# First products of an encoder layer taken from the unnormalised input, with the norm's scale put on their results

## The chip, the cores and the metric

The kernel runs on one core of a Trainium2 chip. The metric is the time on the device in microseconds (us) of one execution. The core has a tensor engine (PE, with its weight loads as PEld), a vector engine (DVE), a scalar engine (ACT), GpSimd (POOL), a sync engine (SP) that here only issues transfers, and DMA queues: those that SP issues on, and those that ACT issues on.

## The reference

Two layers of an encoder over 272 tokens (16 meta tokens and 256 of the input) of width 1024. What matters here is the head of a layer:

```python
def rms_norm(x, gain):
    y = x * lax.rsqrt(jnp.mean(x * x, axis=-1, keepdims=True) + EPS)
    return y * gain

for layer in range(DEPTH):
    hn = rms_norm(h, norm_mix[layer])
    proj = hn @ w_in[layer]        # queries, keys, values, SSM input, pooling input, gates
    ...                            # attention, SSM and pooling, merged: h = h + merged @ w_out
    hn = rms_norm(h, norm_mlp[layer])
    h = h + jnp.square(jax.nn.relu(hn @ w_up[layer])) @ w_down[layer]
return rms_norm(h, norm_final)[:, N_META:]
```

The factor rsqrt(...) is one number for each token, so it can be put on `x * gain` or on the product of `x * gain` with a weight matrix.

## The kernel before

Activations lie transposed: `h` is [128, 8, 272], eight blocks of 128 features by 272 tokens. Every product is made at float32's precision out of three matmuls in a rounded format (fp32r): an operand is split into a rounded part and the rest (`xh` and `xl` for activations, `hi` and `lo` for weights), and `product()` issues hi by xh, hi by xl, lo by xh for each of eight 128x128 blocks, 24 matmuls for a 128x1024 chunk of weights.

`need(i)` serves the weights. It asks for chunks up to three ahead on SP's queue (`raw`, three buffers), and splits up to two ahead: `hi` is an ACT copy (L169), `lo` a DVE subtraction (L170). `proj()` multiplies one chunk of `w_in`: first four SSM input products (results `pju`), then the keys (`pjk`), the values (`pjv`), four query products (`pjq`), pooling inputs, gates. Keys and queries go through a rotation (`rope`, with a small matmul `swk` or `swq`).

The norm at the start (before the loop over layers): five warm-up products (`warm`), the squares of the eight blocks of `h` as they arrive (`sqs`, seven on ACT in L898, one on DVE in L896), and `stats("m0")`: eight products with a matrix of ones add them up over the features (`ss_m`), ACT makes a first 1/sqrt (L294), and three short steps on ACT and DVE refine it (`nx_m`, `nt_m`, L301 `rstd_m`). Then for each block k DVE makes `xn` = h * rstd (L907), ACT `xh` (L908) and DVE `xl` (L912), both with the gain from `vecs`. These stand in program order on DVE by a `pin`, two blocks and then one weight split at a time.

Beside this main stream run generators ("side work") that `pump()` steps through: the SSM's parameters of the first layer are some hundred small DVE operations on 128x32 tiles (`scratch`), followed by wider ones (`gt`, `dd`, `b`); later the SSM scans, attention, pooling. The order of instructions on each engine is fixed when the program is built, by a scheduler that takes priorities and estimates of time; `issue_after` holds side work back until a given instruction. At run time an engine goes through its list in order, and an instruction that waits holds all behind it.

The four results `pju` are copied out of PSUM by ACT (`scaled`, L936, into `ue`) and sent to DRAM (`ud`), from where the scans load them. In the second layer the kernel already takes the first two SSM products before their scale is known: it keeps them (`uk`) and multiplies with rstd on DVE (L940).

Of the kernel before, what the change touches and what calls it, by code (L numbers as in the profile page):

```python
# [20 lines left out]
KT = 8  # L21
# [11 lines left out]
# how the side work is woven into the main stream of products: its rate per slot,  # L33
# by generator and layer, and the slots between a step and the product that uses it
# [23 lines left out]
AHEAD = 3  # chunks of weights loaded ahead of their use  # L58
SPLIT = 2  # and split
WARM = 5  # products that warm the tensor engine up  # L60
# [4 lines left out]
# polynomials, highest power first: e^r on +-ln(2)/2, sine and cosine on +-pi/4  # L65
# [5 lines left out]
# columns of the constant table  # L71
# [3 lines left out]
# columns of the SSM operands of eight groups  # L75
# [9 lines left out]
def encoder(ctx: ExitStack, tc: tile.TileContext, a: dict, out: bass.AP):  # L85
# [5 lines left out]
    class TE:  # L91
        """The tensor engine; side work does not overtake what is written before it."""
# [64 lines left out]
    WHOLE = {(0, 0), (0, 2)}  # (layer, branch) multiplied in float32 without a split  # L157
    raws = []

    def need(i, pinned=False):  # L160
        for j in range(len(raws), min(i + AHEAD + 1, len(chunks))):
            raws.append(wp.tile([P, 8, P], F32, tag="raw", name=f"raw{j}", bufs=3))
            SY.dma_start(raws[j][:, : chunks[j][0].shape[1], :], chunks[j][0])
        for j in range(len(made), min(i + SPLIT + 1, len(chunks))):
# [14 lines left out]
    def first_need(k):  # L179
        """The first chunks, split one by one."""  # L180
        need(k - SPLIT, pinned=True)

# [7 lines left out]
    ORDER = ((0, 1, 2, 3), (2, 3, 0, 1))  # SSM quarters; the last operands made are still on chip  # L190
# [28 lines left out]
    side = []  # L219

    class Side:
        """Steps of a generator, each yielding its cost and the slots it has to wait after it;
        a slot of the main stream allows it `rate`."""
# [24 lines left out]
    def pump(boost=0.0):  # L248
        """Side work for one slot of the main stream."""
        for e in list(side):  # L250
            e.run(boost or e.rate)
# [20 lines left out]
    def feed(n, k, t0):  # L272
        """Scaled, split copy of h's k-th block, and its squares; the last are returned apart."""
# [11 lines left out]
    def stats(name, t0, parts=None):  # L285
        """1/rms of every token, on all partitions; `parts`' squares are still to be summed."""
# [28 lines left out]
    def exp_acc(x):  # L315
        """e^x for x clamped to [-170, 100], to float32's accuracy."""
# [19 lines left out]
    def twice(c, s, co, so, w):  # L336
        """Cosine and sine of twice the angle."""
# [16 lines left out]
    def ssm_params(l):  # L354
# [4 lines left out]
        m5 = st(5)  # mag^4, mag^3, mag^2, mag, 1  # L359
# [49 lines left out]
        ct, sn = st(4), st(4)  # cosines and sines of 1..4 times the angle  # L409
# [12 lines left out]
        # f = (abar - 1) / lambda  # L422
# [13 lines left out]
        # the factors by half quarter and part: f's real part, and its imaginary part signed  # L436
# [3 lines left out]
        # input side: mag^(3-j) e^(-i (j+1) theta) f, rows in the order  # L440
        # (step, quarter, parity, pair), the steps from the last to the first
# [30 lines left out]
        # powers of abar on the output side  # L472
# [15 lines left out]
    def prepare(l, q, bun):  # L488
        """The SSM operands of the groups 8q..8q+7 of layer l."""
# [16 lines left out]
        # rotations by j times the chunk's angle, and the decay of a chunk  # L506
# [15 lines left out]
        # output matrices: [part, group, power, channel]; power 0 is C itself  # L522
# [17 lines left out]
        # input matrices, rows (parity, channel, step), columns (direction, state),  # L540
        # and between them the response within a chunk
# [69 lines left out]
    def prep(l):  # L611
        """Parameters and operands of layer l's SSM, ahead of the layer that uses them."""
# [16 lines left out]
    def scan_quarter(l, q):  # L629
# [22 lines left out]
        # four runs of chunks: real part's halves, imaginary part's halves in reverse  # L652
# [8 lines left out]
        for hb in range(2):  # L661
            # no group crosses the border of a bank
# [18 lines left out]
        # states before each chunk; the chunks run backward on the last 64 partitions  # L681
# [32 lines left out]
        # rotated back, [part, group, chunk], and all chunks put in order  # L714
# [16 lines left out]
        # outputs, rows (parity, step, channel)  # L731
# [23 lines left out]
    cold = []  # quarters whose results are long out  # L755
# [9 lines left out]
    def attention(l, kr, qr, vt, waits):  # L765
# [7 lines left out]
        for gi, (q0, w, mk) in enumerate(groups):  # L773
            yps = pm.tile([P, 512], F32, tag="yps", name=f"yps{l}{gi}", bufs=1)
            n = 4 if w == P else 1
            hw = 2 * w  # columns of two heads
# [103 lines left out]
    with tc.high_priority():  # L880
        params_load(0, S)
        for k in range(4):
            SY.dma_start(h[:, 2 * k : 2 * k + 2, :], a["h0"][:, 2 * k : 2 * k + 2, :])
        S.dma_start(consts[:, C_ONE : C_ONE + P], a["consts"][:, C_ONE : C_ONE + P])
        S.dma_start(vecs, a["vecs"])
        # the tensor engine reaches its full clock while h arrives
# [5 lines left out]
        parts = []  # L892
        sqs = slots(4, "sqs")
        for k in range(KT):
            if k == 1:
                V.tensor_tensor(sqs[:, k], h[:, k], h[:, k], ALU.mult)  # L896
            else:
                S.activation(sqs[:, k], h[:, k], AF.Square)  # L898
            parts.append(sqs[:, k])
        rstd, ia, iv = stats("m0", 0, parts)  # L900
# [416 lines left out]
```

## Time and profile before

| | us |
|---|---|
| median of three runs | 893.82 (893.33 to 897.0) |
| span of the profiled execution | 892.9 |
| PE busy | 870.0 (97%) |
| DVE busy | 675.3 (76%) |
| ACT busy | 541.0 (61%) |
| POOL busy | 4.1 (0%) |

The profiled execution's own time is not among the numbers at hand; its span lies 0.9 us below the median of the runs, which is what start and end take. The page's slices show PE at 9 tenths or more nearly everywhere, with the one low slice at the start; there also DVE and the granted clock are to be read, in microseconds rather than in slices.

### The profile page before, as it was taken

Reading aid. Unit: us, or ns where it says so; the run is one execution under the profiler, and the core shown is the slowest. Engines: PE = TensorE matmul, PEld = TensorE weight load, DVE = VectorE, ACT = ScalarE, POOL = GpSimd, SP = SyncE. Lnnn points to the kernel's source line nnn. Section 1 sums busy time; section 2 is a strip of 40 time slices with the busy share of each in tenths; the row PEclk is TensorE's granted clock in tenths of the full one; section 3 lists DMA queues with packets and bytes.
Section 4 is the critical chain, followed back from the end, with each engine's and each line's share of the span. In section 5 each row is a group of like instructions: output and inputs, shape, how many; then the busy total and the mean of one; then the engine's idle time right before and its main releaser. Section 6 shows DMA issues by size and latency. Waiting matters only on the chain.

```text
span 892.9 us, 18412 instructions
## 1 busy us (share of the span) xinstructions
PE 870.0 (97%) x7174; PEld 814.8 (91%) x7174; DVE 675.3 (76%) x1443; ACT 541.0 (61%) x1005; POOL 4.1 (0%) x32
## 2 busy tenths in 40 slices
PE   6999999999999999999999999999999999999995
PEld 4987777899899999999999988789999999999995
DVE  7987978899986557677896988677878755555564
ACT  5568597845567655477565467575565775357652
POOL 1000000000000000000000000000000000000000
PEclk7999999999999999999999999999999999999998
DMA  7644645454475556958766464625565565555551
GB/s 250 203 154 129 191 117 164 151 159 152 154 228 170 177 169 194 294 187 264 230 201 182 130 215 150 206 96 157 174 192 170 175 193 182 186 185 186 189 189 48
DMA packets 62520, 159.47 MB, mean 179 GB/s; under 512 B 20064, under 2 KB 25952, under 8 KB 62432
## 3 DMA queue, kind: packets, MB, share of 16 engines
q1 hardware_dynamic: 59696, 155.63, 55.8%
q10 hardware_dynamic: 2736, 2.65, 0.9%
q8 instruction: 56, 0.92, 0.4%
q14 instruction: 32, 0.26, 0.1%
HBM read 150.79 MB, written 7.47 MB: 177 GB/s over the span
## 4 chain that ended last, share of the span: by engine, by line
PE 79%; DVE 12%; ACT 4%; DMA 3%; issue 2%; DVEq 0%; ACTq 0%; SPq 0%
PE up L96 21%; PE dn L96 21%; PE pjg L96 10%; PE br L96 5%; PE wo L96 5%; DVE lo L170 3%; PE pju L96 3%; PE s L96 2%; PE pjp L96 2%; PE yps L96 1%; PE pt L101 1%; PE pjq L96 1%; PE l L96 1%; PE tp L96 1%; ACT hi L169 1%
## 5 line engine op out<-in xcount | busy, mean ns | idle before, releaser
L170 DVE TENSOR_TENSOR lo<-raw,hi 128x1024 fp32r<-128x1024 f32 x240 | 292.8, 1221 | 131.4 <-ACT hi L169 128.6
L169 ACT ACTIVATE hi<-raw 128x1024 fp32r<-128x1024 f32 x240 | 253.8, 1058 | 227.6 <-PE dn L96 75.2
L96 PE MATMUL dn<-hid,hi 128*128 128x272 f32 (+1 forms) x1024 | 188.0, 285 | 0.0
L96 PEld LDWEIGHTS dn<-hid,hi 128*128 128x128 f32 x1024 | 159.1, 188 | 0.1
L96 PE MATMUL up<-xh,hi 128*128 128x272 f32 (+1 forms) x512 | 146.2, 286 | 0.0
L96 PE MATMUL dn<-hid,lo 128*128 128x272 f32 (+1 forms) x512 | 146.1, 285 | 0.0
L96 PE MATMUL up<-xh,lo 128*128 128x272 f32 (+1 forms) x512 | 146.0, 285 | 0.0
L96 PE MATMUL up<-xl,hi 128*128 128x272 f32 (+1 forms) x512 | 145.9, 285 | 0.0
L96 PE MATMUL pjg<-xh,hi 128*128 128x272 f32 (+1 forms) x384 | 113.8, 296 | 0.0
L96 PE MATMUL pjg<-xh,lo 128*128 128x272 f32 (+1 forms) x384 | 111.2, 290 | 0.0
L96 PE MATMUL pjg<-xl,hi 128*128 128x272 f32 (+1 forms) x384 | 111.0, 289 | 0.0
L96 PEld LDWEIGHTS up<-xl,hi 128*128 128x128 f32 x512 | 96.3, 188 | 0.5 <-DVE xl L276 0.4
L96 PEld LDWEIGHTS up<-xh,hi 128*128 128x128 f32 x512 | 96.5, 189 | 0.3
L96 PEld LDWEIGHTS up<-xh,lo 128*128 128x128 f32 x512 | 96.6, 189 | 0.0
L96 PEld LDWEIGHTS dn<-hid,lo 128*128 128x128 f32 x512 | 96.5, 188 | 0.0
L96 PEld LDWEIGHTS pjg<-xh,hi 128*128 128x128 f32 x384 | 73.0, 190 | 4.9 <-issue 3.9
L96 PEld LDWEIGHTS pjg<-xh,lo 128*128 128x128 f32 x384 | 73.1, 190 | 2.1 <-issue 2.0
L96 PEld LDWEIGHTS pjg<-xl,hi 128*128 128x128 f32 x384 | 72.9, 190 | 1.8 <-issue 1.5
L96 PE MATMUL wo<-mgh,hi 128*128 128x272 f32 (+1 forms) x128 | 36.6, 287 | 0.6 <-ACT hi L169 0.6
L96 PE MATMUL wo<-mgh,lo 128*128 128x272 f32 (+1 forms) x128 | 36.2, 285 | 0.3 <-DVE lo L170 0.3
L96 PE MATMUL wo<-mgl,hi 128*128 128x272 f32 (+1 forms) x128 | 36.2, 285 | 0.1
L1167 ACT ACTIVATE rs<-re 128x272 f32<-128x272 f32 (+1 forms) x64 | 27.1, 424 | 1.8
(351 smaller groups left out, 1635.9 us busy)
## 6 DMA issues: line engine op xcount, KB each, us to landing
raw<-in_w_in_dram SPq DMA_DIRECT2D x76, 512.0 KB, 3.5
raw<-in_w_up_dram SPq DMA_DIRECT2D x64, 512.0 KB, 4.2
raw<-in_w_dn_dram SPq DMA_DIRECT2D x64, 512.0 KB, 4.0
raw<-in_w_br_dram SPq DMA_DIRECT2D x24, 512.0 KB, 4.0
raw<-in_w_out_dram SPq DMA_DIRECT2D x16, 512.0 KB, 3.7
b<-in_b_row_dram SPq DMA_DIRECT2D x16, 256.0 KB, 5.0
b<-ffd SPq DMA_DIRECT2D x16, 256.0 KB, 4.6
raw<-in_glu_w_dram SPq DMA_DIRECT2D x4, 512.0 KB, 4.3
```

Source lines behind the costliest of these rows:

```text
L96: i = nc.tensor.matmul(*args, **kw)
L101: i = nc.tensor.transpose(*args, **kw)
L169: S.activation(_r(hi), raws[j], AF.Copy)
L170: i_ = V.tensor_sub(_r(lo), raws[j], hi)
L1167: S.activation(sq, re, AF.Square)
```

## The change

Everything is at the start of the first layer.

- The first chunk of weights is requested first on SP's queue, ahead of the four pieces of `h`.
- `rawh` and `rawl` are made from `h` as it comes in: the rounded part of h * gain on ACT and the rest on DVE, the latter pinned. The first four products use them in place of `xh` and `xl`.
- The squares are summed over the eight blocks before the product with ones: ACT squares all eight, GpSimd adds seven times into `ssq`, and one product with ones remains.
- `u0` and `u1` are kept by ACT copies until rstd is there; all four results are multiplied with rstd on DVE (where ACT copied them before).
- `xn`, `xh`, `xl` are still made for all eight blocks, behind rstd, without a pin; keys, values and queries use them.
- `issue_after` and the extra steps of side work at the start (`first_pumps`) are gone.

```diff
-    def need(i, pinned=False):
+    def need(i, pinned=False, load=False):
         for j in range(len(raws), min(i + AHEAD + 1, len(chunks))):
             raws.append(wp.tile([P, 8, P], F32, tag="raw", name=f"raw{j}", bufs=3))
             SY.dma_start(raws[j][:, : chunks[j][0].shape[1], :], chunks[j][0])
+            if load:
+                return None
...
+    rawh, rawl = slots(0, "rawh"), slots(4, "rawl")
     with tc.high_priority():
         params_load(0, S)
+        need(0, load=True)
         for k in range(4):
             SY.dma_start(h[:, 2 * k : 2 * k + 2, :], a["h0"][:, 2 * k : 2 * k + 2, :])
...
-        parts = []
-        sqs = slots(4, "sqs")
+        first_need(0)
         for k in range(KT):
-            if k == 1:
-                V.tensor_tensor(sqs[:, k], h[:, k], h[:, k], ALU.mult)
-            else:
-                S.activation(sqs[:, k], h[:, k], AF.Square)
-            parts.append(sqs[:, k])
-        rstd, ia, iv = stats("m0", 0, parts)
+            S.activation(_r(rawh[:, k]), h[:, k], AF.Copy, scale=gain(0, k))
+            pin(V.scalar_tensor_tensor(
+                _r(rawl[:, k]), h[:, k], gain(0, k), rawh[:, k], ALU.mult, ALU.subtract
+            ))
...
-    ctx.enter_context(tc.issue_after(ia))
...
-    with tc.issue_after(iv):
-        for k in range(0, KT, 2):
-            xn = first(k), first(k + 1)
-            if k < 6:
-                first_need(k // 2)
-            second(k, xn[0])
-            second(k + 1, xn[1])
     Side(prep(0), PREP0)
     pump(BOOST)
-    first_pumps(iv)
+
+    def first_stats():
+        for k in range(KT):
+            if k == 0:
+                S.activation(ssq, h[:, k], AF.Square)
+            else:
+                sq = tmp(f"sq{k}")
+                S.activation(sq, h[:, k], AF.Square)
+                PO.tensor_tensor(ssq, ssq, sq, ALU.add)
+        return stats("m0", 0)[0]
+
+    def normed():
+        for k in range(KT):
+            xn = tmp(f"xn{k}")
+            V.tensor_tensor(xn, h[:, k], rstd, ALU.mult)
+            S.activation(_r(xh[:, k]), xn, AF.Copy, scale=gain(0, k))
+            V.scalar_tensor_tensor(
+                _r(xl[:, k]), xn, gain(0, k), xh[:, k], ALU.mult, ALU.subtract
+            )
...
-            ps = proj(plans[l, "in"][i], name=f"u{q}")
-            if l and i < 2:
+            ps = proj(plans[l, "in"][i], name=f"u{q}", given=xraw)
+            if i < 2:
                 if i == 0:
-                    rstd_l = stats(f"m{l}", 0, [ssq, sq7])[0]
+                    rstd_l = stats(f"m{l}", 0, [ssq, sq7])[0] if l else first_stats()
...
+                    if l == 0:
+                        normed()
```

The order on the engines moves with it. DVE before, at the end of the norm (names as above, `lo` with the number of its tile): the split of the activations starts here, two blocks and one weight split at a time, and the first product can start with it.

```order
L301 SCALAR_TENSOR_TENSOR rstd_m_116<-nt_m_118,rstd_m_116 128x272
L340 TENSOR_SCALAR scratch<-scratch 128x32
L424 TENSOR_TENSOR scratch<-scratch 128x32
L907 TENSOR_TENSOR xn_126<-h,rstd_m_116 128x272
L907 TENSOR_TENSOR xn_129<-h,rstd_m_116 128x272
L170 TENSOR_TENSOR lo_137<-raw_132,hi_136 128x1024
L912 SCALAR_TENSOR_TENSOR xl<-xn_126,vecs,xh 128x272
L912 SCALAR_TENSOR_TENSOR xl<-xn_129,vecs,xh 128x272
```

DVE after, behind the same refinement of rstd: three weight splits and the eight `rawl` stand ahead of this; here come the fourth weight split, the two kept results `ue` and the first `xn`, with parameter work between them.

```order
L303 SCALAR_TENSOR_TENSOR rstd_m_302<-nt_m_304,rstd_m_302 128x272
L418 TENSOR_TENSOR scratch<-scratch 128x32
L172 TENSOR_TENSOR lo_316<-raw_225,hi_315 128x1024
L419 TENSOR_TENSOR scratch<-scratch 128x32
L943 TENSOR_TENSOR ue_358<-uk_310,rstd_m_302 128x4x68
L421 TENSOR_TENSOR scratch<-scratch 128x32
L943 TENSOR_TENSOR ue_362<-uk_356,rstd_m_302 128x4x68
L422 TENSOR_TENSOR scratch<-scratch 128x32
L921 TENSOR_TENSOR xn_366<-h,rstd_m_302 128x272
```

DVE after, at the end of the split of the activations: the last `xl` has moved behind the sixth weight split of the program (`lo_437`) and the third `ue`; before, all eight `xl` stood ahead of the fourth weight split.

```order
L923 SCALAR_TENSOR_TENSOR xl<-xn_390,vecs,xh 128x272
L921 TENSOR_TENSOR xn_394<-h,rstd_m_302 128x272
L943 TENSOR_TENSOR ue_429<-pju_398,rstd_m_302 128x4x68
L172 TENSOR_TENSOR lo_437<-raw_399,hi_436 128x1024
L923 SCALAR_TENSOR_TENSOR xl<-xn_394,vecs,xh 128x272
L943 TENSOR_TENSOR ue_464<-pju_433,rstd_m_302 128x4x68
L172 TENSOR_TENSOR lo_476<-raw_434,hi_475 128x1024
```

PE after, at the change from the keys' product to the values': six matmuls of the values have moved ahead of the keys' last block, whose middle matmul takes the last `xl`; before, the 24 of the keys stood ahead of the 24 of the values.

```order
L96 MATMUL pjv0_506<-xh_70,hi5_436 128x272
L96 MATMUL pjk0_472<-xh_70,hi4_401 128x272
L96 MATMUL pjv0_506<-xl_71,hi5_436 128x272
L96 MATMUL pjv0_506<-xh_70,lo5_437 128x272
L96 MATMUL pjv0_506<-xh_70,hi5_436 128x272
L96 MATMUL pjv0_506<-xl_71,hi5_436 128x272
L96 MATMUL pjv0_506<-xh_70,lo5_437 128x272
L96 MATMUL pjk0_472<-xl_71,hi4_401 128x272
L96 MATMUL pjk0_472<-xh_70,lo4_402 128x272
L96 MATMUL pjv0_506<-xh_70,hi5_436 128x272
```

## Rows read from the trace of the kernel before

**Rows 1.** The page: busy times with share and instructions, then the granted clock in slices.
```profile
PE 870.0 (97%) x7174; PEld 814.8 (91%) x7174; DVE 675.3 (76%) x1443; ACT 541.0 (61%) x1005; POOL 4.1 (0%) x32
PEclk7999999999999999999999999999999999999998
```

**Rows 2.** Waits of PE: operation, releaser; us idle, times, longest.
```profile
PE pju L96 <- ACT xh L908: 7.0, 1, 7.0
...
PE yps L96 <- ACT pts L833: 1.4, 2, 0.9
...
PE y L96 <- ACT st L729: 1.2, 2, 0.7
```

**Rows 3.** Stretches: us, engines' busy time (instructions), granted clock, DMA share, GB/s.
```profile
9.00:11.00 2.00, 0.03 (x1) 0.00 (x0) 2.00 (x23) 1.64 (x4) 0.00 (x0) 1.00 1.01 393
11.00:16.00 5.00, 0.00 (x0) 0.00 (x0) 5.00 (x39) 2.10 (x4) 0.00 (x0) 0.52 0.83 279
16.00:21.00 5.00, 4.43 (x17) 3.95 (x18) 5.00 (x10) 3.51 (x11) 0.11 (x1) 0.50 0.45 120
...
42.00:46.00 4.00, 4.00 (x32) 3.90 (x31) 2.81 (x5) 1.79 (x3) 0.00 (x0) 1.00 0.64 175
46.00:50.00 4.00, 4.00 (x32) 3.91 (x30) 2.65 (x5) 1.77 (x4) 0.00 (x0) 1.00 0.52 178
```

**Rows 4.** Timeline of PE: start, us, operation, count [idle before it].
```profile
16.04 0.82 PE L96 MATMUL pju<-xh,hi 128*128 128x272 f32 x2 [7.00 <-ACT xh L908]
...
31.21 0.29 PE L96 MATMUL pjk<-xh,hi 128*128 128x272 f32 x1
...
34.11 0.29 PE L96 MATMUL pjk<-xh,lo 128*128 128x272 f32 x1
...
37.97 0.29 PE L96 MATMUL pjq<-xh,hi 128*128 128x272 f32 x1
```

**Rows 5.** Timeline of DVE, same columns.
```profile
4.19 0.43 DVE L896 TENSOR_TENSOR sqs<-h 128x272 f32<-128x272 f32 x1
...
8.46 0.28 DVE L546 TENSOR_TENSOR dd<-dvec,consts 16x128 f32<-16x128 f32 x1 [0.69 <-DMA dvec<-in_d_vec_dram]
...
9.70 0.17 DVE L328 TENSOR_SCALAR scratch<-scratch 128x32 f32<-128x32 f32 x1
...
22.17 0.91 DVE L912 SCALAR_TENSOR_TENSOR xl<-xn,vecs,xh 128x272 fp32r<-128x272 f32 x2
22.99 0.79 DVE L907 TENSOR_TENSOR xn<-h,rstd_m 128x272 f32<-128x272 f32 x2
...
25.62 0.28 DVE L478 TENSOR_TENSOR gt<-scratch 64x128 f32<-64x128 f32 x1
...
33.36 2.36 DVE L170 TENSOR_TENSOR lo<-raw,hi 128x1024 fp32r<-128x1024 f32 x2
```

**Rows 6.** All instructions on tile ue: durations in ns, times of first and last.
```profile
L940 DVE TENSOR_TENSOR ue<-uk,rstd_m x2: 640/642/644, 481.5 to 482.0; 128x272 f32<-128x272 f32 x2
```

**Rows 7.** Timeline of ACT, and the issue of the vectors on its queue.
```profile
1.65 0.45 ACTq L885 DMA_DIRECT2D vecs<-in_vecs_dram  x1
...
6.45 1.64 ACT L898 ACTIVATE sqs<-h 128x272 f32<-128x272 f32 x4 [1.07 <-DMA h<-in_h_dram]
9.07 0.49 ACT L294 ACTIVATE rstd_m<-ss_m,eps 128x272 f32<-128x272 f32 x1 [0.98 <-PE ss_m L96]
...
11.69 1.06 ACT L169 ACTIVATE hi<-raw 128x1024 fp32r<-128x1024 f32 x1 [0.18 <-DMA raw<-in_w_in_dram]
```

**Rows 8.** DMA issues: queue, count, KB each, median us to landing.
```profile
vecs<-in_vecs_dram ACTq DMA_DIRECT2D x1, 38.0 KB, 5.0
```

**Rows 9.** Timeline of POOL, same columns.
```profile
0.76 0.32 POOL L888 MEMSET warm<- 128x272 f32 x1
...
18.04 0.11 POOL L520 MEMSET b<- 128x8 f32 x1 [15.18 <-ACT b L519]
```

**Rows 10.** Timeline of SP's queue: the third scan's load.
```profile
119.31 1.29 SPq L642 DMA_DIRECT2D ub<-ud  x2
```

More of the change, by code (lines that the diff above doesn't have):

```diff
@@ L891, in encoder @@
             TE.matmul(ps[:, :NT], warm[:, 0, :P], warm[:, 0], start=True, stop=True)
-        parts = []
-        sqs = slots(4, "sqs")
+        first_need(0)
         for k in range(KT):
-            if k == 1:
-                V.tensor_tensor(sqs[:, k], h[:, k], h[:, k], ALU.mult)
-            else:
-                S.activation(sqs[:, k], h[:, k], AF.Square)
-            parts.append(sqs[:, k])
-        rstd, ia, iv = stats("m0", 0, parts)
+            S.activation(_r(rawh[:, k]), h[:, k], AF.Copy, scale=gain(0, k))
+            pin(V.scalar_tensor_tensor(
+                _r(rawl[:, k]), h[:, k], gain(0, k), rawh[:, k], ALU.mult, ALU.subtract
+            ))
     S.dma_start(consts[:, :C_ONE], a["consts"][:, :C_ONE])
     S.dma_start(consts[:, C_J:], a["consts"][:, C_J:])
-    ctx.enter_context(tc.issue_after(ia))
-    def first(k):
-        xn = tmp(f"xn{k}")
-        pin(V.tensor_tensor(xn, h[:, k], rstd, ALU.mult))
-        S.activation(_r(xh[:, k]), xn, AF.Copy, scale=gain(0, k))
-        return xn
-    def second(k, xn):
-        pin(V.scalar_tensor_tensor(_r(xl[:, k]), xn, gain(0, k), xh[:, k], ALU.mult, ALU.subtract))
-    with tc.issue_after(iv):
-        for k in range(0, KT, 2):
-            xn = first(k), first(k + 1)
-            if k < 6:
-                first_need(k // 2)
-            second(k, xn[0])
-            second(k + 1, xn[1])
     Side(prep(0), PREP0)
     pump(BOOST)
-    first_pumps(iv)
+    def first_stats():
[15 more added lines that the diff above has]
+            )
     for l in range(DEPTH):
@@ L927, in encoder @@
         N = NT - t0
-        xs = [(xh[:, k, :], xl[:, k, :]) for k in range(KT)]
+        xall = [(xh[:, k, :], xl[:, k, :]) for k in range(KT)]
+        xraw = [(rawh[:, k, :], rawl[:, k, :]) for k in range(KT)] if l == 0 else None
         xc = [(xh[:, k, t0:], xl[:, k, t0:]) for k in range(KT)]
@@ L940, in scaled, with proj @@
                 V.tensor_tensor(o, ps, r, ALU.mult)
-        def proj(i, full=True, name=""):
+        def proj(i, full=True, name="", given=None):
             ps = mm_tile(f"pj{name}{l}")
+            xs = given or xall
             n = NT if full else N
@@ L976, in encoder @@
             pump()
+        if l == 0:
+            rstd = None
         qk = slots(2, f"qk{l}")
```

## The prediction

> **What bounds the kernel now.** First the page: PE is busy for 97% of the span and full in nearly every slice, so a gain can only come from time in which PE waits [rows 1]. The waits of PE come next: one of 7.0 us stands out, before the first product, which waits for the first `xh`; the next longest that the change could touch are 1.4 and 1.2 us in all and lie far behind [rows 2]. Then the stretches around it: PE does nothing from 9.0 to 16.0, the granted clock falls to half in that time, and it still stands at 0.50 from 16 to 21, after PE had been idle [rows 3]. That is the time the change is after. But in the same rows DVE is busy for 2.00 of 2.00, 5.00 of 5.00 and 5.00 of 5.00 us. So the start is bounded by DVE's list, and what PE waits for is a place in that list. I therefore follow the list, to the point where the old and the new program ask the same of it.
>
> **That point** is the first query product. Behind it the rows of both programs on PE, DVE and ACT are the same but for a few leftovers. It starts at 37.97 before [rows 4]. The time after it I take over unchanged: PE is the bound there, and DVE has room (2.81 of 4.00 and 2.65 of 4.00 us busy [rows 3]), about 2.5 us in eight, for the 1.6 us of small work that the change pushes behind that point (four `gt`, `dd`, the fourth `ue`). So the change is worth what it does to 37.97.
>
> **What PE gains at its head.** `rawl` needs no norm, so the first product can start some 8 us earlier. This lead does not last: the four SSM products also need four weight splits, and the fourth of them stands behind the refinement of rstd on DVE now. By the sum below DVE ends that split at about 24.5, and 24 matmuls later, at 0.126 each (31.21 to 34.11 is 23 of them [rows 4]), PE is through at 27.6, against 31.2 before: a lead of 3.6 us. Then the keys come, and they need `xl`.
>
> **DVE's list up to the last `xl`.** Before, the row of two weight splits begins at 33.36 and takes 2.36 [rows 5], so the sixth split ends at 34.5. Up to there DVE had done, by the lists of instructions, what it must now do up to the last `xl`: the same parameter work, eight `xn`, eight `xl`, six splits. What differs:
> - plus eight `rawl`, each as an `xl`: two of these take from 22.17 to 22.99 [rows 5], so 8 x 0.41 = 3.3;
> - plus three `ue`: 0.64 for the same operation in the second layer [rows 6], less 0.08 by which neighbours overlap (two `xn` take 0.79, not two times 0.43 [rows 5]), 3 x 0.56 = 1.7;
> - plus `nx`, which was ACT's: a short step over 272 columns, 0.3 by the 0.35 that a step of 0.43 takes in sequence;
> - less the one square (0.35 in sequence), four `gt` (0.28 each, 0.20 in sequence, 0.8), `dd` (0.2) and the 0.7 for which `dd` kept DVE waiting on its vector [rows 5].
>
> That is 34.5 + 3.3 + 1.7 + 0.3 - 0.35 - 0.8 - 0.2 - 0.7 = 37.8, with no wait counted.
>
> **From the last `xl` to the query product.** Before, from the last matmul of the keys at 34.11 to 37.97 there are 25 matmuls and the small `swk` pair: 3.86, of which 25 x 0.126 = 3.15 are matmuls and 0.7 the pair [rows 4]. Now 20 matmuls and the pair stand behind the last `xl`: 0.1 + 20 x 0.126 + 0.7 = 3.3. The query product starts at 41.1 at the earliest: **3.1 us later** than before. The lead is spent waiting for `xl`.
>
> **The wait for the norm.** This is the step that no row of before shows, since no add ran on GpSimd. DVE comes to the first weight split where it came to the row at 9.70, less the square, the wait and `dd`: 8.4 [rows 5]. A split (1.14), eight `rawl`, 17 small operations at 0.105, a split, 20 small, a split and two small bring it to `nx` at 19.3. ACT makes the second chunk's `hi` when it has landed, at 11.7 [rows 7] (weights and `h` only change places in the queue, so the bytes ahead of it are the same; `vecs` is issued at 1.65 and takes 5.0 [rows 7, 8], so the eight `rawh` are done by then), then one square, another `hi` and a square: the first add can start at about 13.9. Seven adds follow one another. Each lies between 0.43, DVE's price for two inputs of this size [rows 5], and 0.96, three times GpSimd's memset of this size (0.32 [rows 9]) for two reads and a write; I take 0.70, the middle, with 0.1 between two. The adds end at 19.5, the product with ones and its way to DVE take 0.7, so DVE waits from 19.3 to 20.2: 0.9 (bounds 0 and 2.7). Then `nt` waits for ACT, which between its two steps of 0.49 [rows 7] and 0.43 now also has three or four short ones: another 0.9. Together **1.8 us** (0 to 3.6), all of it ahead of the last `xl`.
>
> The Trainium skill ("GPSIMD Engine Reference", section 3.1) gives about 2.6 cycles an element for an add of two tensors on GpSimd, by which I estimate 0.65 us an add and a sum lower by 0.35; no row here shows it. [...]
>
> **The clock.** PE now has 24 keys' matmuls and a few of the values', some 3.8 us of work, spread over the 11 to 12 us in which it waits for `xl`. Rows 3 show the granted clock at 0.52 and 0.50 after a full idle stretch; they don't show it for scattered work. If it falls there, the last 20 matmuls and a little more run at half speed, 20 x 0.126 = 2.5 us more. I take 1.0 (bounds 0 and 2.4). At the head the reverse, a clock that stays up since PE idles less, changes nothing, as DVE sets the pace.
>
> **Other edits.** Weights first: `h` lands later by 512 KB at 393 GB/s [rows 3], 1.3 us, hidden behind DVE's parameter work, which needs no `h`. The later `ue` go out to DRAM some microseconds later; the load of the third scan stands at 119.31 [rows 10], far behind. Seven fewer products with ones: they lay in PE's idle time, worth nothing. ACT loses four copies and gains eight `rawh` and two `uk`, and idles in that stretch (3.51 of 5.00 busy [rows 3]).
>
> **Sum.** 3.1 + 1.8 + 1.0 = 5.9. The profiled span of 892.9 becomes 898.8, and with the 0.9 that lies between that span and the median of 893.8: 899.7. Bounds: 3.1 + 0 + 0 gives 896.9, and 3.1 + 3.6 + 2.4 gives 902.9.
>
> **Rivals.**
> 1. *GpSimd holds DVE up.* If an add and a DVE operation with two inputs cannot run side by side, seven adds take 7 x 0.70 = 4.9 us out of DVE, of which 1.8 were waits anyway: 3.1 more, 902.8. No row shows the two engines together. The Trainium skill ("SBUF — State Buffer", section "Who interferes with whom") speaks for it: by its rule a DVE instruction with two inputs in SBUF contends with a GpSimd instruction that reads SBUF, and the second of them is blocked for the whole of the first. Against it: DVE then has many operations of one input, and an add may be the one that waits.
> 2. *The loss is absorbed.* No wait for the norm, the clock stays up, and of the 2.6 us that PE waits later [rows 2] 1.0 goes, because work beside it is further on: 893.8 + 3.1 - 1.0 = 895.9, within half a per cent.
> 3. *The lead holds* (faster). DVE's busy time before may hold time that isn't its own, as `xl` was pinned behind weight splits that had waited for ACT's `hi`; without the pin it may get through the list sooner. It decides where the last `xl` is done by 37.97 - 3.3 = 34.7 instead of 37.8; with the whole lead of 3.6 kept, 890.2. Against it: the splits stand without idle time ahead of them in DVE's timeline.
>
> **Chances.** Forecast 0.53, rival 1 0.2, rival 2 0.21, rival 3 0.06. Half a per cent, 4.5 us, is about what a measurement of this kernel can tell from no change: faster is below 889.3, slower above 898.3. Rival 3 keeps 0.04 below the lower bound. The part of the forecast between 896.9 and 898.3 is some 0.09, so "same" has 0.21 + 0.02 + 0.09 = 0.32, slower the remaining 0.64. The range: from 895.0, a little under rival 2, to 904.5, somewhat over the upper bound of 902.9, since rival 1 with adds of 0.96 would pass it.
>
> **What would show it.** In the profile after, the first product starts near 8 to 9 us; DVE is full from 8 to 42 but for a wait of `nx` for `ss_m` near 19 and a short one of `nt`; the first query product starts at 42 to 44, PE waiting in between for `xl` in several pieces; GpSimd's adds take 0.6 to 0.8 each. The forecast is wrong if the last `xl` is out before 37 (then the list was miscounted), if small DVE operations stretch while the adds run (rival 1), or if, with the query product late by 5 us, the span is not (then something later gives it back).

## The result, and the profile after

The change makes the kernel slower: 901.25 us (median of four runs, 900.18 to 902.83) against 893.88 before, a ratio of 1.0082 with a 95% interval of 1.0057 to 1.0107. The forecast was 899.7 with a range of 895.0 to 904.5.

The profiled execution of the changed kernel took 902.83 us with a span of 901.0. So about 1.8 us lie around the span, and not the 0.9 that I took. In every execution on record, those of the kernel before among them, it is 1.7 to 2.1; so the execution that was profiled before stands some 0.8 above its median, and this one stands 1.6 above. The spans differ by 8.1, the medians by 7.4.

The page after (answers to [rows 1]): GpSimd's busy time has grown by the adds to 10.7 us, from 4.1, and DVE's by 10 us.

```profile
PE 872.5 (97%) x7160; PEld 816.1 (91%) x7160; DVE 685.2 (76%) x1455; ACT 543.7 (60%) x1011; POOL 10.7 (1%) x39
```

The waits of PE after (us in total, times, longest; answers to [rows 2]): the one wait of 7.0 us for `xh` is gone, and in its place stand four of 1.6 to 3.3 us in all, for the parts of the split and for a weight split, up to the keys.

```profile
PE pju L96 <- DVE lo L172: 3.3, 1, 3.3
PE pju L96 <- DVE rawl L900: 3.0, 1, 3.0
PE pjk L96 <- ACT xh L922: 2.8, 2, 2.3
...
PE pju L96 <- ACT rawh L899: 1.6, 1, 1.6
```

Stretches after (columns as in [rows 3]): DVE is full from 9 to 21 here too. PE has work from 11 to 16, but at a granted clock of 0.50, and is idle for most of 16 to 21 and of 35 to 38; there the clock falls again, to 0.50 between 38 and 42.

```profile
11.00:16.00 5.00, 4.90 (x21) 4.90 (x22) 5.00 (x15) 4.67 (x10) 2.05 (x3) 0.50 0.86 298
16.00:21.00 5.00, 1.73 (x11) 1.50 (x10) 5.00 (x15) 1.26 (x2) 4.59 (x5) 0.84 0.05 13
...
35.00:38.00 3.00, 0.91 (x3) 0.48 (x3) 2.93 (x14) 0.22 (x1) 0.00 (x0) 0.79 0.89 246
38.00:42.00 4.00, 3.38 (x12) 2.83 (x12) 4.00 (x10) 1.87 (x4) 0.00 (x0) 0.50 0.11 30
```

PE's timeline after (answers to [rows 4]): the first product starts at 7.66, 8.4 us earlier than before, and its second matmul only at 11.10. The last `xl` is used at 43.15, and the first query product starts at 46.30, against 37.97 before: 8.3 us late. From there to the end of the span it takes 854.7 us, before 854.9. So by net the whole difference of the spans arises ahead of that point; in between it grows once, to 9.7 at the last step of the SSM (`gl`, 236.1 against 226.4), and falls back in the second layer.

```profile
7.66 0.39 PE L96 MATMUL pju<-rawh,hi 128*128 128x272 f32 x1 [1.62 <-ACT rawh L899]
11.10 0.60 PE L96 MATMUL pju<-rawl,hi 128*128 128x272 f32 x1 [3.05 <-DVE rawl L900]
...
38.62 0.60 PE L96 MATMUL pjk<-xh,hi 128*128 128x272 f32 x1 [2.29 <-ACT xh L922]
...
43.15 0.43 PE L96 MATMUL pjk<-xl,hi 128*128 128x272 f32 x1
...
46.30 0.29 PE L96 MATMUL pjq<-xh,hi 128*128 128x272 f32 x1
```

DVE's timeline after (answers to [rows 5]). Between 13.8 and 20.9 seven operations on 128x32 tiles take 0.75 to 0.79 us, where their neighbours take 0.17 to 0.19; three of the seven are shown. The line 41.94 is the last `xl`.

```profile
4.76 0.18 DVE L320 TENSOR_SCALAR scratch<-scratch 128x32 f32<-128x32 f32 x1 [3.87 <-DMA scratch<-in_lam_dram]
...
9.41 1.22 DVE L172 TENSOR_TENSOR lo<-raw,hi 128x1024 fp32r<-128x1024 f32 x1
10.55 3.39 DVE L900 SCALAR_TENSOR_TENSOR rawl<-h,vecs,rawh 128x272 fp32r<-128x272 f32 x8
13.85 0.75 DVE L325 TENSOR_SCALAR scratch<-scratch 128x32 f32<-128x32 f32 x1
14.51 0.17 DVE L330 TENSOR_SCALAR scratch<-scratch 128x32 f32<-128x32 f32 x1
14.60 0.18 DVE L396 SCALAR_TENSOR_TENSOR scratch<-scratch 128x32 f32<-128x32 f32 x1
14.70 0.79 DVE L327 SCALAR_TENSOR_TENSOR scratch<-scratch 128x32 f32<-128x32 f32 x1
...
16.59 0.78 DVE L334 CAST scratch<-scratch 128x32 int32<-128x32 f32 x1
...
24.26 0.44 DVE L300 TENSOR_SCALAR nx_m<-ss_m 128x272 f32<-128x272 f32 x1
...
25.20 0.44 DVE L302 SCALAR_TENSOR_TENSOR nt_m<-nt_m,nx_m 128x272 f32<-128x272 f32 x1 [0.32 <-ACT nt_m L301]
...
41.94 0.50 DVE L923 SCALAR_TENSOR_TENSOR xl<-xn,vecs,xh 128x272 fp32r<-128x272 f32 x1
42.35 0.63 DVE L943 TENSOR_TENSOR ue<-pju,rstd_m 128x272 f32<-128x272 f32 x1
```

GpSimd's adds, from the timeline and from the list of instructions on `ssq` (ns, shortest, median, longest): seven adds in the 7.1 us in which DVE has seven long operations. The last line is the second add by itself: it ends at 15.44, and DVE's second long operation, which starts at 14.70, at 15.49.

```profile
13.79 7.11 POOL L915 TENSOR_TENSOR ssq<-ssq,sq 128x272 f32<-128x272 f32 x7 [10.93 <-ACT sq L914]
...
L915 POOL TENSOR_TENSOR ssq<-ssq,sq x7: 767/808/1750, 13.8 to 19.2; 128x272 f32<-128x272 f32 x7
...
14.64 0.80 POOL L915 TENSOR_TENSOR ssq<-ssq,sq 128x272 f32<-128x272 f32 x1
```

### The profile page after: what moved, and what is told of

Same layout as the page of the kernel before. It is cut to its first block, busy times and chain, and to the rows that moved or that the text cites. A ratio compares the mean times of both kernels' runs of the same rounds, so it can differ in the third digit from the quotient of the medians.

```text
span 901.0 us, 18420 instructions
## 1 busy us (share of the span) xinstructions
PE 872.5 (97%) x7160; PEld 816.1 (91%) x7160; DVE 685.2 (76%) x1455; ACT 543.7 (60%) x1011; POOL 10.7 (1%) x39
## 4 chain that ended last, share of the span: by engine, by line
PE 57%; DVE 5%; DMA 3%; ACT 2%; issue 1%; SPq 0%; DVEq 0%; ACTq 0%
PE dn L96 21%; PE up L96 21%; PE pjg L96 4%; PE wo L96 3%; PE br L96 2%; DVE lo L172 1%; PE pju L96 1%; PE s L96 1%; DMA yq<-yd 1%; PE pjp L96 1%; DMA yd<-yt 1%; ACT hi L171 1%; DMA raw<-in_w_br_dram 1%; PE yps L96 1%; PE tp L96 1%
## 5 line engine op out<-in xcount | busy, mean ns | idle before, releaser
L1193 DVE TENSOR_TENSOR db<-dn,rq 128x272 f32<-128x272 f32 (+1 forms) x32 | 13.8, 433 | 19.4 <-PE dn L96 19.3
```

The lines of the kernel that those rows point to most:

```text
L1193: V.tensor_tensor(tb, ps, rq[:, t0:], ALU.mult)
```

## The experiments

The theory after this reading: DVE's list up to the last `xl` sets the first query product, as forecast, but the list was lengthened by seven stops, one for each add on GpSimd (theory A, rival 1 of the prediction). The rival (B): the adds hurt only as a chain that the norm waits for. Each time is a median; ratios are against runs of the kernel before on the same chip.

**Products with ones instead of adds.** The first cut of the edit keeps the step `nx` on DVE, as in the changed kernel.

```diff
-        if len(parts) > 2:
+        if len(parts) > 8:
...
+        sqs = slots(1, "sqs")
         for k in range(KT):
-            if k == 0:
-                S.activation(ssq, h[:, k], AF.Square)
-            else:
-                sq = tmp(f"sq{k}")
-                S.activation(sq, h[:, k], AF.Square)
-                PO.tensor_tensor(ssq, ssq, sq, ALU.add)
-        return stats("m0", 0)[0]
+            S.activation(sqs[:, k], h[:, k], AF.Square)
+        return stats("m0", 0, [sqs[:, k] for k in range(KT)])[0]
```

> The changed kernel, but the eight squares are summed by eight products with ones, as before the change, and GpSimd adds nothing. In the trace of the changed kernel seven small DVE operations take 0.75 to 0.79 us instead of 0.18, all of them between 13.8 and 20.9, while the seven adds run. Theory A (each add blocks DVE once): those seven are short again, 7 x 0.58 = 4.1 us less on DVE ahead of the last xl, and 0.4 less waiting for the norm. The first query product moves from 46.3 to about 41.8, the time from 901.2 to about 896.8. Rival B (the adds matter only as a chain that the norm waits for, and the long operations have another cause): DVE's wait for the norm is 0.1 and 0.3 in the changed kernel, so at most 0.4 is to be had: about 900.8.

Measured: 898.75 us, ratio 1.0059 (1.0040 to 1.0078). No operation on DVE is long any more, but DVE now waits 1.15 us for the norm. The last two `xl` begin at 36.03, so that the last is done some 5.5 us earlier than in the changed kernel; the query product, at 44.13, is only 2.2 earlier. In the order that the scheduler built here the fifth weight split stands behind the sixth `xl`, and PE waits for it in one piece with 46 matmuls still to come.

```profile
20.94 0.44 DVE L300 TENSOR_SCALAR nx_m<-ss_m 128x272 f32<-128x272 f32 x1 [1.15 <-ACT rstd_m L296]
...
34.89 1.22 DVE L172 TENSOR_TENSOR lo<-raw,hi 128x1024 fp32r<-128x1024 f32 x1
36.03 0.91 DVE L919 SCALAR_TENSOR_TENSOR xl<-xn,vecs,xh 128x272 fp32r<-128x272 f32 x2
```

PE's timeline of the same kernel:

```profile
36.16 0.60 PE L96 MATMUL pjk<-xh,lo 128*128 128x272 f32 x1 [6.96 <-DVE lo L172]
...
44.13 0.29 PE L96 MATMUL pjq<-xh,hi 128*128 128x272 f32 x1
```

Of the 4.4 that A gave some half came; by the trace the rest went to the wait for the norm and to the order behind it. The intervals of the two ratios, here and for the changed kernel, overlap, so that this run alone does not settle what the adds cost; the next does.

**The adds, with nobody waiting for them.** This is the kernel above with seven GpSimd adds into a tile that is not read.

```diff
             S.activation(sqs[:, k], h[:, k], AF.Square)
+            if k == 1:
+                PO.tensor_tensor(ssq, sqs[:, 0], sqs[:, 1], ALU.add)
+            elif k > 1:
+                PO.tensor_tensor(ssq, ssq, sqs[:, k], ALU.add)
```

> As the kernel with products with ones, but GpSimd still does the seven adds, into a tile that nobody reads; the norm does not depend on them. Theory A (each add blocks DVE once): seven operations of DVE are long again while the adds run, and nearly all that the products with ones gained is lost: about 900.5. Rival B (the chain through the adds): nobody waits for them, so the time is that of the kernel without adds.

Measured: 901.41 us, on the same chip, 2.7 more than without the adds, ratio 1.0087 (1.0070 to 1.0105); the slowest of the four without adds took 899.9, the fastest of the four with them 900.87. The list of DVE is otherwise that of the kernel above; seven of its small operations are long again, and the query product starts at 46.97 instead of 44.13, 2.8 us later. This decides for A: the norm here doesn't depend on the adds. Seven stops of some 0.6 are 4.1 us; 1.15 of that were DVE's wait for the norm in the kernel without adds, which is gone here, and 0.2 an earlier start, so about 2.8 remain, as measured. Two of the seven lines, between short neighbours, and then the adds:

```profile
15.68 0.17 DVE L334 CAST scratch<-scratch 128x32 int32<-128x32 f32 x1
15.77 0.77 DVE L398 TENSOR_SCALAR scratch<-f 128x32 f32<-128x32 f32 x1
16.45 0.18 DVE L327 SCALAR_TENSOR_TENSOR scratch<-scratch 128x32 f32<-128x32 f32 x1
16.55 0.17 DVE L400 TENSOR_SCALAR scratch<-scratch 128x32 f32<-128x32 f32 x1
16.64 0.79 DVE L399 TENSOR_TENSOR f<-f,scratch 128x32 f32<-128x32 f32 x1
```

```profile
13.99 0.77 POOL L913 TENSOR_TENSOR ssq<-sqs 128x272 f32<-128x272 f32 x1 [11.13 <-ACT sqs L911]
14.83 6.64 POOL L915 TENSOR_TENSOR ssq<-ssq,sqs 128x272 f32<-128x272 f32 x6
```

**The parameters requested first.**

```diff
-        params_load(0, S)
+        params_load(0, SY)
         need(0, load=True)
```

> The changed kernel, with the SSM's parameters (48 KB, for which DVE's first operation waits) requested on SP's queue ahead of the first weights, not on ACT's queue beside them. Theory: the first weights ahead of everything made DVE start at 4.76 instead of 3.89, and DVE's list sets the time of the first query product; with the parameters first DVE starts near 3.9 and the time falls by 0.9, to 900.3. Rival: the weights land later by the same, and DVE waits for them at its first weight split: 901.2, no change.

Measured: 900.83 us, ratio 1.0089 (1.0052 to 1.0125): no change that can be told from none. The mechanism is not the rival's: DVE starts by 2.8 instead of 4.76 and its first weight split is at 6.86 instead of 9.41. The last `xl` is done at 39.15, 3.3 us earlier. What took the gain back is, by the trace, the order that came with it: PE waits 3.2 us for the seventh add and 7.4 us for the fifth weight split, which again stands behind the sixth `xl`; the query product starts at 46.43. Two lines of the waits of PE:

```profile
PE pjk L96 <- DVE lo L172: 7.4, 1, 7.4
PE ss_m L96 <- POOL ssq L915: 3.2, 1, 3.2
```

**The weights requested behind h again.**

```diff
         params_load(0, S)
-        need(0, load=True)
         for k in range(4):
             SY.dma_start(h[:, 2 * k : 2 * k + 2, :], a["h0"][:, 2 * k : 2 * k + 2, :])
+        need(0, load=True)
```

> The changed kernel with the first weights requested behind h again, as before the change. The first weight split and the eight rawl stand some 15 small operations later on DVE. Theory (DVE's list sets the time, what comes first in it does not matter): DVE starts near 3.9 instead of 4.8, the first product comes later, the first query product at the same time or 0.9 earlier: 900.3 to 901.2. Rival (weights first is what makes the start early enough): the adds and the norm come later by the 2 to 3 us that the weights land later, and so does the query product: about 903.5.

Measured: 904.41 us, ratio 1.0094 (1.0061 to 1.0126). PE's first product waits until 13.26 for the weights' `hi`, 4.6 us for the adds, and the query product starts at 49.65, 3.4 us later than in the changed kernel. Theory as I had put it (what comes first on DVE's list does not matter) is wrong: the adds begin at 17.47 and not at 13.79, and the norm comes later with them. DVE's first operation starts at 4.23 here, with no weights requested ahead of its parameters. Requesting the weights first is the part of the change that helps, by the trace; the two ratios, 1.0094 and 1.0082, are too near to show it.

```profile
PE ss_m L96 <- POOL ssq L915: 4.6, 1, 4.6
```

**The clock in PE's wait.** This adds 40 matmuls that nobody reads to the kernel with products with ones, between the fourth SSM product and the keys.

```diff
+        if l == 0:
+            fill = aux_tile("fill")
+            for _ in range(40):
+                TE.matmul(fill[:, :NT], _r(rawh[:, 0, :P]), _r(rawh[:, 0]), start=True, stop=True)
         qk = slots(2, f"qk{l}")
```

> The kernel with products with ones, and 40 matmuls whose result nobody reads between the fourth SSM product and the keys, where PE waits 7.0 us for a weight split and the granted clock is 0.50 from 35 to 38 and 0.80 from 38 to 42. They take 40 x 0.126 = 5.0 us of that wait. Theory (the clock that fell in the wait costs time behind it): the keys start at 36.2 as there, at full clock, and the 46 matmuls up to the first query product take 6.3 instead of 8.0 us: 1.7 less, 897.0. Rival (behind the wait DVE's list decides, not PE): the query product and the time stay, 898.7.

Measured: 901.59 us, ratio 1.0067 (1.0046 to 1.0089), on another chip than the kernel without the filling, whose ratio was 1.0059. In the trace the theory holds as far as the query product: the keys go on at 36.20 as there, the granted clock is 1.00 instead of 0.50 and 0.80, and the query product starts at 42.57 instead of 44.13, 1.6 earlier. The time does not show it; the ratios are the same within their intervals. In the traces 1.4 us of the lead are still there at the last query product of the second layer (512.9 against 514.3), and at that layer's last gate product it is 3.7 behind (664.3 against 660.6). The edit adds nothing there; what made that stretch longer in the one execution profiled is open.

```profile
28.79 4.94 PE L96 MATMUL fill<-rawh 128*128 128x272 f32 x38
...
36.20 0.40 PE L96 MATMUL pjk<-xh,lo 128*128 128x272 f32 x1 [2.23 <-DVE lo L172]
...
42.57 0.29 PE L96 MATMUL pjq<-xh,hi 128*128 128x272 f32 x1
```

**The last `xl` moved ahead.**

```diff
-                        normed()
+                        with tc.high_priority():
+                            normed()
```

> The changed kernel, but xn, xh and xl are put at high priority, so that on DVE the last xl stands ahead of some 15 small and 12 wider operations on SSM parameters and of the sixth weight split, 5 to 5.5 us of work by the trace of the changed kernel. Theory (the last xl in DVE's list sets the first query product, and DVE has room behind it): the last xl ends near 37 instead of 42.4, the query product starts near 41, and the time falls by about 5, to 896. Rival (DVE has no room for it): the work that moves back is waited for later, by the weight splits behind it, and the time stays within 1 us of 901.2.

Measured: 900.74 us, ratio 1.0086 (1.0064 to 1.0109), the same as the changed kernel. The query product did come earlier, at 42.55, by 3.75, and in the trace most of that is kept: the first gate product starts 3.6 ahead (73.23 against 76.85), `gl` 4.2 ahead (231.9 against 236.1), and the span is 898.3 against 901.0. PE waits for a gate for 1.2 us at 130 us. The medians do not show the lead. The execution profiled here was the fastest of its four, that of the changed kernel the slowest of its four, so the two spans say little of the medians. So neither the theory nor the rival (that the work moved back is waited for) is shown, and what became of the lead is open. The first gate product in the changed kernel and in this one, and the wait:

```profile
76.85 0.29 PE L96 MATMUL pjg<-xh,hi 128*128 128x272 f32 x1
```

```profile
73.23 0.29 PE L96 MATMUL pjg<-xh,hi 128*128 128x272 f32 x1
```

```profile
PE br L96 <- ACT gates L1062: 1.2, 1, 1.2
```

The first matmul of the first SSM output (`y`), which the expectation of the three edits goes by, is no good mark for this: it starts at 122.00, 79.5 behind the query product, where it was 77.4 behind in the changed kernel (123.72), but between 42 and 128 us PE waits for only 0.5 in all, so the output has only moved back in PE's order.

**The change carried through the whole layer.** `xh` and `xl` hold the split without the norm, rstd is put on the rope tables, values, pooling inputs and gates; squares by products with ones, parameters first.

```diff
-    rawh, rawl = slots(0, "rawh"), slots(4, "rawl")
+    rawh, rawl = xh, xl
...
-                    if l == 0:
-                        normed()
...
-        if l == 0:
-            rstd = None
-
         qk = slots(2, f"qk{l}")
```

> The change carried through the whole first layer, as the second layer already does it: the split of x without its norm goes into xh and xl themselves, xn and the second split are gone, rstd stays and is put on the rope tables (two DVE operations), the values, the pooling inputs and the 24 gates (one DVE multiplication each, about 0.43). The squares are summed by products with ones and the SSM's parameters are requested first, as in two kernels before. Theory (DVE's list up to the first query product sets the time, and DVE has room behind it): 16 operations of about 0.38 go from the list, 6.1 us, three of 0.4 come; together with the 2.5 that products with ones gained the first query product comes at about 36 to 37, some 9 us earlier than in the changed kernel, and the gates' 10 us on DVE are hidden: about 892. Rival (DVE has no room there): the 10 us of gates are waited for, and the time is 897 to 902.

Measured: 898.66 us, ratio 1.0047 (1.0028 to 1.0066). The start is better than forecast: the query product at 33.81, 4.2 us ahead of the kernel before. At the first gate product the lead is 4.0 (64.52 against 68.56), and the last step of the SSM (`gl`) starts at 227.88 against 226.37 before, 1.5 behind. The time is the rival's. What the trace shows of its reason: between 34 and 228 us ACT waits 6.6 us for the gates that DVE multiplies by rstd now, where before it took them from PE; and PE waits 1.3 us for a weight split of DVE, at 168 us, and 1.7 for attention (before: none and 0.4), and behind the first of these the granted clock is 0.71 from 170 to 175. That DVE is full there is not shown: it is busy for 172.2 of those 194 us, before for 170.4. At the MLP's first product this kernel is 3.1 behind the one before (275.6 against 272.5); of the reasons for that, these waits and the clock are what the trace shows.

```profile
ACT gates L1055 <- DVE gates L1054: 6.6, 5, 2.8
...
PE yps L96 <- ACT pts L835: 1.7, 2, 1.1
...
PE pjg L96 <- DVE lo L172: 1.3, 1, 1.3
```

**Only the products up to the queries raw.** As the last, with the raw split in its own tiles, and the normed split made behind the queries, for pooling inputs and gates. Values and queries get the same `given` as the keys.

```diff
+            if given and not full:
+                x_ = [(a_[:, t0:], b_[:, t0:]) for a_, b_ in given]
...
-        urgent(rope(proj(plans[l, "in"][4], name="k"), kr, 0, f"k{l}"))
+        urgent(rope(proj(plans[l, "in"][4], name="k", given=xraw), kr, 0, f"k{l}"))
...
+        if l == 0:
+            normed()
+            rstd = None
         side_att = Side(attention(l, kr, qr, vt, list(waits)), (ATT0, ATT1)[l])
```

> The first products' raw split is used for keys, values and queries too (rstd goes onto the rope tables and the values, four short DVE operations in all), and the normed split is made behind the queries, for pooling inputs and gates, which need no scaling then; squares by products with ones, parameters first. Theory (up to the query product as the kernel that is raw throughout, 33.8; behind it the gates cost nothing more, only the eight xn and xl, 6 us, between the queries and the first SSM output): the lead of 4 us shrinks to 1 to 3 by the first SSM output near 115 us and stays from there: 891 to 893. Rival (DVE is short between 45 and 115 us by all of what is pushed there): 896 to 898, as the kernel raw throughout.

Measured: 898.64 us (894.87 to 903.6), ratio 1.0063 (1.0032 to 1.0094); four of the eight executions took under 896 (granted clock of the whole span 0.990 to 0.992), and the other four, the one profiled among them with 901.6, took 901.6 to 903.6 (0.982 to 0.985). In it the query product starts at 33.78, but the first pooling product waits 3.8 us for the late `xh`, until 52.71 (before it starts at 52.30), and the granted clock is 0.71 from 46 to 60 and 0.82 from 60 to 85. In this execution the lead is gone before 60 us: I had not counted that PE reaches the pooling inputs before the late split is made.

```profile
PE pjp L96 <- ACT xh L918: 3.8, 1, 3.8
```

**Three edits together:** products with ones, parameters first, `xl` ahead.

```diff
-        params_load(0, S)
+        params_load(0, SY)
...
-                PO.tensor_tensor(ssq, ssq, sq, ALU.add)
-        return stats("m0", 0)[0]
+        return stats("m0", 0, [sqs[:, k] for k in range(KT)])[0]
...
-                        normed()
+                        with tc.high_priority():
+                            normed()
```

> Three edits on the changed kernel together: squares summed by products with ones, SSM parameters requested first, xn, xh and xl at high priority. In the order built from it the fifth weight split stands among the xl, where the kernels with only one of the first two edits have it behind the sixth. Theory (the query product follows DVE's list, and what is pushed behind is paid only where the SSM's scan needs it): the query product comes at about 35 to 36, 2 to 3 us before that of the kernel before; of that lead some 3 us go again ahead of the first SSM output near 115 us, as in the kernel with xl first: 892 to 895. Rival (the start decides alone): 890 to 891.

Measured: 894.87 us (891.38 to 903.13), ratio 1.0009 (0.9977 to 1.0041): 6 us better than the change, and the same as the kernel before. The query product starts at 36.92, 1.1 us ahead of it. Five of the ten executions took 891.38 to 893.14, and the one profiled 896.6. In it the first gate product still starts 1.0 ahead (67.52 against 68.56); at 124 us PE waits 1.2 us for a gate, after it the granted clock is 0.66 for 15 us, and `gl` starts 4.1 behind (230.5 against 226.4). So it is there that this execution loses its lead. No trace shows one of the five shorter ones; on record is that their granted clock, over the whole span, was 0.992 to 0.995, and that of the five longer ones 0.984 to 0.990:

```profile
115.00:125.00 10.00, 8.45 (x80) 5.16 (x79) 7.76 (x12) 9.03 (x21) 0.12 (x1) 1.00 0.32 94
125.00:140.00 15.00, 15.00 (x72) 11.29 (x71) 8.31 (x24) 9.47 (x21) 0.00 (x0) 0.66 0.52 155
```

**The same, with the scans woven in earlier** (the rate `SCAN0` from 2.0 to 2.6), to take away that wait.

```diff
-SCAN0 = 2.0
+SCAN0 = 2.6
```

> The kernel with the three edits together, with the rate of the first layer's SSM scans raised from 2.0 to 2.6, so that their steps are woven in earlier. In the trace of the three edits PE waits 1.2 us for a gate near 124 us (on ACT the gate stands behind a scan's and attention's steps), and the granted clock is at 0.65 from 125 to 140; its runs fall in two groups, 891.4 to 893.1 and 896.6 to 897.9. In the order built now that gate stands ahead of the scan's steps. Theory (that wait brings the clock down and makes the upper group): the upper group goes, the median is 891 to 893. Rival (earlier scan steps make another wait on PE): 894 to 898, with a wait of over 1 us for a scan or for attention in that region.

Measured: 895.67 us, ratio 1.0015 (0.9995 to 1.0035). The rival holds: the gate's wait is gone, and PE waits for attention instead, 1.3 us at 125 and 4.9 in the whole run, with the clock again at 0.66 from 125 to 140. By its median no version here beats the kernel before.

```profile
PE yps L96 <- ACT pts L835: 4.9, 6, 1.3
```

## Why the prediction was right, point by point

The number came out in the range in part by luck: the wait that the forecast added did not come, and the stops that it had put among the rivals came in its place.

**The bound** was read rightly: DVE's list up to the last `xl`, and from there to the first query product. The time behind that point was indeed the same by net (854.7 and 854.9), for this change. The kernels with more work pushed back show that this was no general truth: by their traces three of them (raw throughout, late split, three edits) lose their lead between 46 and 230 us. Nor is it always the last `xl` that counts: with products with ones, and with the parameters first, PE waited for a weight split in DVE's list.

**The sum**, however, comes out near for partly other reasons. It gave 5.9 at the query product; measured are 8.3 in the profiled execution, and 7.4 between the medians. By its own terms:

- The list. DVE's first weight split was to come at 8.4 and came at 9.41. The step that failed is "weights first is hidden behind DVE's parameter work": that work itself waits for a transfer, the parameters, and DVE starts on them at 4.76 instead of 3.89 (the row before stands below this list), 0.9 of the 1.0. How much of that the 512 KB requested beside them cost is not settled: with the weights behind `h` again DVE starts at 4.23, and in the four other traces with the weights ahead and the parameters on ACT's queue at 4.39 to 4.62. From that split to the end of the last `xl` I had worked out 29.4; measured are 32.9, of which 4.1 are the stops at the adds and 0.4 waits for the norm, so the list itself was 1.0 shorter than worked out.
- The wait for the norm, 1.8 forecast, was 0.4. The adds took about as long as I took (0.77 at the shortest, 0.70 taken; 0.89 from one start to the next, 0.8 taken, and the last held to 1.75 by a weight split), but DVE came to `nx` at 24.26 and not at 19.3, since the adds held it up on the way: what I priced as a wait for the adds was paid during the adds.
- The stops, 7 x 0.58 = 4.1, are rival 1, which had a chance of 0.2 and a price of 3.1 on top. It is what happened. The Trainium skill ("SBUF — State Buffer", section "Who interferes with whom") had the rule for operations with two inputs in SBUF; the trace agrees, with 0.75 to 0.79 in place of 0.18 once for each add. My reasons against it didn't hold: operations with one input (the `TENSOR_SCALAR` and `CAST` above) were stopped too, which the rule as I had put it left out, and with one exception it was DVE that waited, and not the add.
- From the last `xl` to the query product 3.95 instead of 3.3; the 0.65 I put down to the clock (0.50 from 38 to 42), where 1.0 was taken.

DVE's first operation on the parameters, from its timeline before, which no group above has; the row after stands further up:

```profile
3.89 0.18 DVE L318 TENSOR_SCALAR scratch<-scratch 128x32 f32<-128x32 f32 x1 [2.99 <-DMA scratch<-in_lam_dram]
```

Together 3.1 + 1.0 + 4.1 + 0.4 - 1.0 + 0.65 = 8.25 of the measured 8.33. The forecast held because the missed stops and the late start (5.1) stand against a norm wait, a list and a clock that were priced too high (1.4, 1.0 and 0.35), and because the range took rival 1 in. The median of 901.25 lies halfway between the forecast's 899.7 and rival 1's 902.8; it is the trace, and the run with adds that nobody waits for, that decide for the rival.

**The lead of PE** is as told: the first product starts at 7.66, and all of it is spent waiting for DVE. But the fourth SSM product ends at 32.4, not 27.6, so there was no lead of 3.6 to lose. DVE's fourth weight split ends at 28.4 and not at 24.5, by the late start and the stops; PE does not even wait for it, since from 20.3 to 26.2 the granted clock is 0.50, which the forecast had put at nothing for the head. By the forecast's own sum, 24 matmuls at 0.126 behind that split, PE would have been through at 31.4; the other 1.0 I put down to the clock.

**Rival 2** (absorbed) and **rival 3** (the lead holds) did not happen in the change itself. The three edits together show that the change's idea can be brought back to no loss, and the kernel that is raw throughout shows that a lead of 4 us at the query product is possible but does not last.

**The other edits** show no cost of their own in the traces but the late start above, and weights first is worth something to this version: without it the query product is 3.4 later.

## What to carry to other kernels

When one engine is idle, look for the list that it waits for before moving work: here PE's 7 us could only be had by shortening DVE's list, and the change lengthened it. Work given to an idle GpSimd is not free if DVE is the bound, since each GpSimd add here stopped one DVE operation for some 0.6 of its 0.8 us; eight small matmuls on the idle PE were the cheaper sum. A lead at the start is not a gain yet: one wait of 1.2 us at 124, with the lower clock behind it, took more than the lead of the three edits. Look for where the work that was pushed back is waited for next, and follow the lead through several marks, since a mark that has moved in the order misleads.

## What the runs showed of the hardware

A 128x272 add of two SBUF operands on GpSimd takes 0.77 us at the shortest, and the next starts 0.08 behind it. The 128x32 operation of DVE that meets an add, whether it has one or two inputs, ends 0.05 us behind the add, some 0.6 late; the two or three small operations before it, around the start of the add, take their usual 0.17 to 0.19. The other way round, a weight split of 1.21 us on DVE holds the add that starts behind it: the longest took 1.75 us here and 1.95 with the idle adds. The first add starts 0.08 us behind the end of its square (13.71), after 10.9 us in which GpSimd had nothing to do, so that nothing else is seen to hold it up; what a first add costs without such a pause no run shows.
